# Running sums of the SSD scan: spread over the partitions by DMA from DRAM instead of by picking products

## The chip, the cores and the metric

The kernel runs on one core of a Trainium2 chip. The metric is the device time of one execution in microseconds (us). Five engines run side by side, each with its own instruction stream: TensorE (PE in the profile; PEld is its weight load), VectorE (DVE), ScalarE (ACT), GpSimd (POOL) and SyncE (SP), which here issues every DMA.

## The reference

A decoder trunk of two layers for one sequence of 256 tokens and 1024 features. Each layer is a SwiGLU feed-forward block, a token mixer and a second feed-forward block, each behind an RMSNorm that is scaled and shifted by the conditioning vector. The mixer of layer 0 is a latent attention, that of layer 1 the SSD scan (Mamba-2), in two chunks of 128 tokens, with 32 heads in 4 groups. What the change touches is the decay inside the scan:

```
a = (dt * A)                                  # per chunk, group, head, token
a_cum = jnp.cumsum(a, axis=-1)
seg = a_cum[..., :, None] - a_cum[..., None, :]
decay_ls = jnp.exp(jnp.where(causal, seg, -jnp.inf))
cb = jnp.einsum('bclgn,bcsgn->bcgls', Cc, Bc)
y_diag = jnp.einsum('bcgls,bcgkls,bcsgkp->bclgkp', cb, decay_ls, xdt)
decay_to_end = jnp.exp(a_cum[..., -1:] - a_cum)
states = jnp.einsum('bclgn,bcgkl,bclgkp->bcgkpn', Bc, decay_to_end, xdt)
```

## The kernel before

Features lie on the 128 partitions and the 256 tokens along the free dimension. Every product with a weight is made of three matmuls in float32r: weights and activations are each split into a rounded part and a remainder (`mm3`), so that a projection to 128 outputs is 8 x 3 = 24 matmuls of 256 columns.

Weights come by DMA from SyncE into five raw buffers of 1 MB (`prefetch`, line 184); a raw buffer holds two pieces for two projections. ScalarE casts a piece to float32r (`whi`, line 206) and VectorE subtracts to get the remainder (`wlo`, line 207). `piece` traces these splits two pieces ahead of the projection that uses them; five `whi` and five `wlo` buffers bound how far the engines can run ahead. Between them VectorE also forms the conditioning vectors from further weight loads (line 237).

The program is traced in Python order, and a planner then orders each engine's stream by readiness, with the trace order as priority. `order` (`keep_in_program_order`) pins an instruction behind everything traced before it on its engine, and `matmul` does so while `pin` is set, as it is inside the steps of the scan.

Work tiles: `slot` gives [128, 512] tiles from a ring of NSLOT = 30. They hold the layer's inputs (8), the second set of normalised inputs (8), the activations of a feed-forward block (22), and in the SSD layer convolution outputs, gates and scan tiles. `bank` gives one of the 8 PSUM banks.

The SSD layer (`ssd`) runs 40 projections of `win` in the order SSD_ORDER and, between them, steps of two generators. `ssd_dt` computes dt, a and the running sums; it ends with the sums by token in `nac`, `acol` and `ate`, and with the sums by head as rows in `acr`: 64 rows, where rows 0 to 31 hold a rounded value and rows 32 to 63 the remainder, with 64 rows of zeros below. Then `ssd_group` runs for each group of 8 heads in four pairs. For pair `i`, `decay` spreads the two heads' rows over all 128 partitions with two matmuls whose weight is a column of `s_pick` (a matrix that adds row h and row 32 + h), broadcast to 128 columns, into a PSUM bank. `decay_next` (line 1278) takes an exponential of the second chunk for the carried state, `decay_cut` (line 1286) takes the minimum with the own column, which masks, into a slot, and `decay_exp` (line 1297) takes four more exponentials into the `dec` tile. `times_cb` (line 1301) multiplies by C.B, `ymm` makes the products with x.dt, and `leave` (line 1316) adds the skip term. `decay(i + 1)` is traced ahead of `decay_next(i + 1)` by one step; a step is half a projection. The Exp and Silu functions need different activation tables on ScalarE, each change of which is an ACT_TABLE_LOAD.

`gate` works on a group's outputs when its scan is done and its z projections are there. Its sums of squares (line 1452) and scales (line 1463) lead to the inputs of the output projection in `down`.

Of the kernel before, what the change touches and what calls it, by code (L numbers as in the profile page):

```python
# [7 lines left out]
F32 = mybir.dt.float32  # L8
F32R = mybir.dt.float32r
# [3 lines left out]
ALU = mybir.AluOpType  # L13
# [3 lines left out]
T = 256  # L17
# [11 lines left out]
NSLOT = 30  # L29
# [35 lines left out]
class Trunk:  # L65
    def __init__(self, ctx, tc, a, out):
# [3 lines left out]
            tc.tile_pool(name="ps", bufs=8, space=bass.MemoryType.PSUM))  # L70
        self.uid = 0
# [1054 lines left out]
    def ssd_setup(self):  # L1126
        nc = self.nc
# [12 lines left out]
        self.pick = self.const([128, 32], "s_pick", F32R)  # L1140
        nc.gpsimd.memset(self.pick[64:128].bitcast(F32), 0.0)
        self.acr = self.const([128, T], "acr", F32R)
        nc.gpsimd.memset(self.acr[64:128].bitcast(F32), 0.0)
        self.order(nc.vector.tensor_tensor(out=self.pick[0:64], in0=self.ident[0:64, 0:32], in1=self.ident[0:64, 32:64], op=ALU.add))
# [17 lines left out]
    def ssd_dt(self, ps, R):  # L1162
# [27 lines left out]
        for n in (13, 9, 5, 1):  # L1190
# [13 lines left out]
        av = self.const([128, 2, 2, 32], "a_f")  # L1204
        nc.vector.tensor_tensor(
            out=av, in0=self.dt.rearrange("p c (o h) -> p c o h", o=1).broadcast_to([128, 2, 2, 32]),
            in1=self.nega.rearrange("p (c o h) -> p c o h", c=1, o=1).broadcast_to([128, 2, 2, 32]), op=ALU.mult)
        yield
        ah = self.const([128, 2, 2, 32], "a_h", F32R)
        al = self.const([128, 2, 2, 32], "a_l", F32R)  # L1210
# [6 lines left out]
        for c in range(2):  # L1217
            o = pc[:, c * 32:(c + 1) * 32]
            self.matmul(o, self.tri, ah[:, c, 0], start=True, stop=False)
            self.matmul(o, self.tri, al[:, c, 0], start=False, stop=True)  # L1220
        o = pc[:, 64:96]
        self.matmul(o, self.onesr, ah[:, 0, 0], start=True, stop=False)
        self.matmul(o, self.onesr, al[:, 0, 0], start=False, stop=True)
        pr = self.bank()
        for c in range(2):
            o = pr[0:64, c * 128:(c + 1) * 128]
            self.matmul(o, ah[:, c].rearrange("p o h -> p (o h)"), self.tri, start=True, stop=False)
            self.matmul(o, al[:, c].rearrange("p o h -> p (o h)"), self.tri, start=False, stop=True)
# [9 lines left out]
        nc.vector.tensor_copy(out=self.acr[0:64], in_=pr[0:64, 0:T])  # L1238
        nc.vector.tensor_tensor(out=self.acr[32:64], in0=pr[32:64, 0:T], in1=self.acr[32:64].bitcast(F32),
# [377 lines left out]
```

## Time and profile before

| what | value |
|---|---|
| median of 3 runs | 1082.81 us (1082.79 to 1084.13) |
| the profiled execution: its time | 1082.82 us |
| the profiled execution: its span | 1081.1 us |
| TensorE busy | 1063.7 us (98%) |
| VectorE busy | 871.5 us (81%) |
| ScalarE busy | 628.5 us (58%) |
| DMA | 259.59 MB, mean 240 GB/s |

The span runs from the first instruction to the last; some 1.7 us of the time lie around it. In the rows, L1286 is line 1286 of the kernel, `out<-in` names the tiles without their buffer numbers, `128x512 f32<-128x512 f32` are the shapes, and `xN` counts instructions. `[0.60 <-DVE dec L1301]` is idle time of the engine before the instruction and what ended it. Matmul records overlap, so their durations do not add up to time. The SSD layer lies between about 690 and 900 us of the span, the scan's four groups between 737 and 856 us.

### The profile page before, as it was taken

The numbers are of one execution on the slowest core, as the hardware profiler recorded it, in microseconds if no ns is written. First come the engines' busy times: TensorE is split into PE (matmuls) and PEld (weight loads), VectorE is DVE, ScalarE is ACT, GpSimd is POOL, SyncE is SP. The second block draws the span as 40 slices with busy tenths as digits, with TensorE's granted clock in tenths as the row PEclk, the third lists the DMA queues.
The fourth block names the chain that finished last, engine by engine and source line by source line (L and its number), as shares of the span: only waits on it lengthen the run. The fifth ranks groups of instructions, "written<-read, shape, count | busy, mean of one in ns | idle before, by whom it ended". The sixth has DMA issues, their size and how long they took to land.

```text
span 1081.1 us, 21734 instructions
## 1 busy us (share of the span) xinstructions
PE 1063.7 (98%) x8814; PEld 1046.8 (97%) x8814; DVE 871.5 (81%) x1551; ACT 628.5 (58%) x1106; POOL 42.1 (4%) x102
## 2 busy tenths in 40 slices
PE   7999999999999999999999999999999999999998
PEld 6999999999999999999999999999999899999998
DVE  5899988889989878767989886599997788756642
ACT  5564544478658444444745444498898767544431
POOL 0000000000100000100000000000211000000000
PEclk9999999999999999999999999999999999999999
DMA  8999998853366888865699987534344455566630
GB/s 342 355 357 347 336 373 298 296 202 135 117 235 226 319 313 312 300 231 211 240 346 357 343 318 250 170 142 161 114 137 156 157 179 211 203 217 215 229 132 21
DMA packets 38264, 259.59 MB, mean 240 GB/s; under 512 B 4370, under 2 KB 5522, under 8 KB 8084
## 3 DMA queue, kind: packets, MB, share of 16 engines
q1 hardware_dynamic: 38164, 258.21, 65.5%
q8 instruction: 69, 1.13, 0.4%
q14 instruction: 31, 0.25, 0.1%
HBM read 257.14 MB, written 1.05 MB: 239 GB/s over the span
## 4 chain that ended last, share of the span: by engine, by line
PE 92%; DMA 3%; DVE 3%; ACT 1%; issue 0%; SPq 0%; ACTq 0%
PE bank L295 91%; DMA raw<-in_adao_dram 3%; PE bank L300 1%; DVE raw L259 1%; DMA raw<-in_xt_dram 0%; DVE wlo L613 0%; ACT sl L808 0%; ACT t L1020 0%; DVE wlo L207 0%; ACT whi L206 0%; DVE sl L1463 0%; DVE ssq L942 0%; ACT t L937 0%; DVE mx L1015 0%; ACT sl L806 0%
## 5 line engine op out<-in xcount | busy, mean ns | idle before, releaser
L295 PE MATMUL bank<-sl,whi 128*128 128x256 f32 (+2 forms) x5360 | 957.2, 282 | 4.0 <-ACT sl L647 2.8
L295 PEld LDWEIGHTS bank<-sl,whi 128*128 128x128 f32 (+1 forms) x5360 | 819.7, 188 | 7.7 <-ACT sl L647 3.6
L295 PE MATMUL bank<-sl,wlo 128*128 128x256 f32 (+2 forms) x2680 | 747.6, 281 | 0.9 <-DVE wlo L207 0.9
L206 ACT CAST whi<-raw 128x1024 fp32r<-128x1024 f32 (+1 forms) x329 | 341.5, 1041 | 326.0 <-PE bank L295 230.8
L295 PEld LDWEIGHTS bank<-sl,wlo 128*128 128x128 f32 (+1 forms) x2680 | 504.5, 189 | 1.2 <-DVE wlo L207 1.1
L207 DVE TENSOR_TENSOR wlo<-raw,whi 128x1024 fp32r<-128x1024 f32 (+1 forms) x329 | 397.8, 1213 | 99.5 <-ACT whi L206 96.4
L237 DVE SCALAR_TENSOR_TENSOR raw<-raw,cb 128x1024 f32<-128x1024 f32 x128 | 154.4, 1218 | 14.2 <-DMA raw<-in_adaw_dram 14.1
L329 ACT CAST sl<-t 128x256 fp32r<-128x256 f32 x125 | 48.6, 404 | 23.4 <-DVE t L521 16.4
L330 DVE TENSOR_TENSOR sl<-t,sl 128x256 fp32r<-128x256 f32 x125 | 50.8, 417 | 1.0 <-ACT sl L329 0.7
L460 DVE SCALAR_TENSOR_TENSOR x<-bank,mod,x 128x256 f32<-128x256 f32 x48 | 22.9, 480 | 22.2 <-PE bank L295 21.8
L521 DVE TENSOR_TENSOR t<-t,bank 128x256 f32<-128x256 f32 x70 | 28.7, 416 | 14.8 <-PE bank L295 14.8
L1159 DVE SCALAR_TENSOR_TENSOR sl<-t,cst,sl 128x256 f32<-128x256 f32 x72 | 34.6, 490 | 0.2
L410 ACT ACTIVATE sl<-x,scol 128x256 fp32r<-128x256 f32 x40 | 20.3, 508 | 23.5 <-DVE x L460 23.4
L520 ACT ACTIVATE t<-bank 128x256 f32<-128x256 f32 x70 | 26.0, 380 | 0.0
L409 POOL CAST sl<-bspl 128x4 fp32r<-128x4 f32 x40 | 12.7, 365 | 319.2 <-PE bank L295 232.4
L440 POOL TENSOR_TENSOR rr<-rv,mhalf 128x2 f32<-128x2 f32 x11 | 12.7, 1154 | 308.0 <-DVE rv L436 308.0
L259 DVE SCALAR_TENSOR_TENSOR raw<-raw,cb 128x1024 f32<-128x1024 f32 x16 | 19.5, 1222 | 5.9 <-DMA raw<-in_adao_dram 5.9
L295 PE MATMUL bank<-whi,sl 128*128 128x384 f32 (+1 forms) x80 | 24.3, 368 | 0.0
L1297 ACT ACTIVATE dec<-sl,nac 128x128 f32<-128x128 f32 x64 | 20.5, 394 | 3.6 <-DVE sl L1286 3.5
L411 DVE SCALAR_TENSOR_TENSOR sl<-x,scol,sl 128x256 fp32r<-128x256 f32 x40 | 19.2, 480 | 4.2 <-ACT sl L410 4.1
L423 ACT ACTIVATE t<-t,mod,scol 128x256 f32<-128x256 f32 x32 | 18.2, 595 | 4.2 <-DVE t L422 4.0
L613 DVE TENSOR_TENSOR wlo<-raw,whi 128x1024 fp32r<-128x1024 f32 (+1 forms) x17 | 19.5, 1156 | 0.0
(216 smaller groups left out, 662.0 us busy)
## 6 DMA issues: line engine op xcount, KB each, us to landing
raw<-in_wgu_dram SPq DMA_DIRECT2D x80, 1024.0 KB, 5.2
raw<-in_adaw_dram SPq DMA_DIRECT2D x64, 1024.0 KB, 5.8
raw<-in_wdn_dram SPq DMA_DIRECT2D x44, 1024.0 KB, 6.2
raw<-in_win_dram SPq DMA_DIRECT2D x19, 1024.0 KB, 4.9
raw<-in_wout_dram SPq DMA_DIRECT2D x8, 1024.0 KB, 4.8
raw<-in_wop_dram SPq DMA_DIRECT2D x6, 1024.0 KB, 5.7
raw<-in_adao_dram SPq DMA_DIRECT2D x6, 1024.0 KB, 7.3
raw<-in_mwo_dram SPq DMA_DIRECT2D x4, 1024.0 KB, 4.9
```

What stands on the lines that cost most here:

```text
L206: self.nc.scalar.copy(out=hi, in_=raw)
L207: self.nc.vector.tensor_tensor(out=lo, in0=raw, in1=hi.bitcast(F32), op=ALU.subtract)
L237: nc.vector.scalar_tensor_tensor(out=w, in0=w, scalar=1.0, in1=self.cb, op0=ALU.mult, op1=ALU.mult, accum_out=self.mod[:, q, 2 * u + i:2 * ...
L259: self.order(nc.vector.scalar_tensor_tensor(out=w, in0=w, scalar=1.0, in1=self.cb, op0=ALU.mult, op1=ALU.mult, accum_out=self.mod[:, q, c]))
L295: ins = self.nc.tensor.matmul(*a, **k)
L329: self.nc.scalar.copy(out=hi, in_=src)
L330: self.nc.vector.tensor_tensor(out=lo, in0=src, in1=hi.bitcast(F32), op=ALU.subtract)
L460: nc.vector.scalar_tensor_tensor(out=self.x[m], in0=ps[:, 0:T], scalar=self.mod[:, q, m:m + 1], in1=self.x[m], op0=ALU.mult, op1=ALU.add)
L520: nc.scalar.activation(out=tg, in_=pg[:, 0:T], func=AF.Silu)
L521: nc.vector.tensor_tensor(out=tg, in0=tg, in1=pu[:, 0:T], op=ALU.mult)
L1159: nc.vector.scalar_tensor_tensor(out=dst, in0=u[:, t:t + T], scalar=cw[:, t:t + 1], in1=dst, op0=ALU.mult, op1=ALU.add)
L1297: self.order(nc.scalar.activation(out=t[:, j, 2 * c], in_=q[:, o:o + 128], func=AF.Exp, bias=self.nac[:, c, h:h + 1]))
```

## The change

The running sums by head are no longer split into a rounded value and a remainder in `acr`. `ssd_dt` writes 32 rows of them as float32 to a scratch tensor `acd` in DRAM, by a DMA from SyncE. `row_load(i)` then loads the rows of heads 2i and 2i + 1, 2 KB, broadcast to all 128 partitions, into an SBUF tile `arow`. Four such tiles exist; the first four pairs are loaded at the end of `ssd_dt`, and after the exponentials of a pair the load for the pair four later is issued. `decay` hands out the next of these tiles in place of two matmuls; `decay_cut` writes into it in place of a slot. The column sums in `ssd_dt` are made from a single copy of a. To make room, the ring of slots goes from 30 to 27.

```diff
--- before.py
+++ after.py
@@ -26,7 +26,8 @@
 RAW_BUFS = 5
 W_BUFS = 5
 AHEAD = 2
-NSLOT = 30
+NSLOT = 27
+ROWS = 4
 NDEF = 6
 ZRAW = 13
 SETUP_AT = 15
@@ -68,6 +69,7 @@
         self.p = ctx.enter_context(tc.tile_pool(name="sb", bufs=1))
         self.ps_pool = ctx.enter_context(
             tc.tile_pool(name="ps", bufs=8, space=bass.MemoryType.PSUM))
+        self.dram = ctx.enter_context(tc.tile_pool(name="dr", bufs=1, space=bass.MemoryType.DRAM))
         self.uid = 0
         self.pin = False
 
@@ -1137,11 +1139,7 @@
         nc.vector.tensor_copy(out=self.tri, in_=u)
         self.onesr = self.const([128, 128], "s_onesr", F32R)
         self.order(nc.vector.tensor_copy(out=self.onesr, in_=self.ones))
-        self.pick = self.const([128, 32], "s_pick", F32R)
-        nc.gpsimd.memset(self.pick[64:128].bitcast(F32), 0.0)
-        self.acr = self.const([128, T], "acr", F32R)
-        nc.gpsimd.memset(self.acr[64:128].bitcast(F32), 0.0)
-        self.order(nc.vector.tensor_tensor(out=self.pick[0:64], in0=self.ident[0:64, 0:32], in1=self.ident[0:64, 32:64], op=ALU.add))
+        self.acd = self.dram.tile([32, T], F32, name="acd")
 
     def conv_evac(self, ps, R, j, dst):
         nc = self.nc
@@ -1201,13 +1199,12 @@
         nc.vector.scalar_tensor_tensor(out=p, in0=p, scalar=2.0, in1=z, op0=ALU.mult, op1=ALU.mult)
         nc.vector.scalar_tensor_tensor(out=d, in0=u, scalar=0.0, in1=p, op0=ALU.max, op1=ALU.add)
         self.dt = d.rearrange("p (c h) -> p c h", c=2)
-        av = self.const([128, 2, 2, 32], "a_f")
-        nc.vector.tensor_tensor(
-            out=av, in0=self.dt.rearrange("p c (o h) -> p c o h", o=1).broadcast_to([128, 2, 2, 32]),
-            in1=self.nega.rearrange("p (c o h) -> p c o h", c=1, o=1).broadcast_to([128, 2, 2, 32]), op=ALU.mult)
-        yield
-        ah = self.const([128, 2, 2, 32], "a_h", F32R)
-        al = self.const([128, 2, 2, 32], "a_l", F32R)
+        av = self.const([128, 2, 32], "a_f")
+        nc.vector.tensor_tensor(out=av, in0=self.dt, in1=self.nega.rearrange("p (c h) -> p c h", c=1)
+                                .broadcast_to([128, 2, 32]), op=ALU.mult)
+        yield
+        ah = self.const([128, 2, 32], "a_h", F32R)
+        al = self.const([128, 2, 32], "a_l", F32R)
         nc.vector.tensor_copy(out=ah, in_=av)
         nc.vector.tensor_tensor(out=al, in0=av, in1=ah.bitcast(F32), op=ALU.subtract)
         yield
@@ -1216,16 +1213,16 @@
         pc = self.bank()
         for c in range(2):
             o = pc[:, c * 32:(c + 1) * 32]
-            self.matmul(o, self.tri, ah[:, c, 0], start=True, stop=False)
-            self.matmul(o, self.tri, al[:, c, 0], start=False, stop=True)
+            self.matmul(o, self.tri, ah[:, c], start=True, stop=False)
+            self.matmul(o, self.tri, al[:, c], start=False, stop=True)
         o = pc[:, 64:96]
-        self.matmul(o, self.onesr, ah[:, 0, 0], start=True, stop=False)
-        self.matmul(o, self.onesr, al[:, 0, 0], start=False, stop=True)
+        self.matmul(o, self.onesr, ah[:, 0], start=True, stop=False)
+        self.matmul(o, self.onesr, al[:, 0], start=False, stop=True)
         pr = self.bank()
         for c in range(2):
-            o = pr[0:64, c * 128:(c + 1) * 128]
-            self.matmul(o, ah[:, c].rearrange("p o h -> p (o h)"), self.tri, start=True, stop=False)
-            self.matmul(o, al[:, c].rearrange("p o h -> p (o h)"), self.tri, start=False, stop=True)
+            o = pr[0:32, c * 128:(c + 1) * 128]
+            self.matmul(o, ah[:, c], self.tri, start=True, stop=False)
+            self.matmul(o, al[:, c], self.tri, start=False, stop=True)
         yield
         self.nac = self.const([128, 2, 32], "nac")
         nc.vector.tensor_scalar(out=self.nac, in0=pc[:, 0:64].rearrange("p (c h) -> p c h", c=2), scalar1=-1.0,
@@ -1235,9 +1232,16 @@
                               in_=pc[:, 0:64].rearrange("p (c h) -> p c h", c=2))
         self.ate = self.const([128, 32], "ate")
         nc.vector.tensor_tensor(out=self.ate, in0=pc[:, 64:96], in1=self.nac[:, 0], op=ALU.add)
-        nc.vector.tensor_copy(out=self.acr[0:64], in_=pr[0:64, 0:T])
-        nc.vector.tensor_tensor(out=self.acr[32:64], in0=pr[32:64, 0:T], in1=self.acr[32:64].bitcast(F32),
-                                op=ALU.subtract)
+        acr = self.t1()[0:32]
+        nc.vector.tensor_copy(out=acr, in_=pr[0:32, 0:T])
+        nc.sync.dma_start(out=self.acd, in_=acr)
+        self.rows = [self.row_load(i) for i in range(ROWS)]
+
+    def row_load(self, i):
+
+        t = self.p.tile([128, 2 * T], F32, name=self.name("arow"), tag="arow", bufs=ROWS)
+        self.nc.sync.dma_start(out=t, in_=self.acd[2 * i:2 * i + 2].rearrange("h l -> (h l)").partition_broadcast(128))
+        return t
 
     def ssd_group(self, g, BT, CT, xsT):
 
@@ -1262,12 +1266,7 @@
             return t
 
         def decay(i):
-            ps = self.bank()
-            for j in range(2):
-                h = 8 * g + 2 * i + j
-                self.matmul(ps[:, j * T:(j + 1) * T], self.pick[:, h:h + 1].broadcast_to([128, 128]),
-                                 self.acr, start=(j == 0), stop=(j == 1))
-            return ps
+            return self.rows.pop(0)
 
         def decay_next(i, ps):
 
@@ -1281,13 +1280,12 @@
 
         def decay_cut(i, ps):
 
-            q = self.slot()
             h = 8 * g + 2 * i
-            nc.vector.tensor_tensor(out=q.rearrange("p (j c l) -> p j c l", j=2, c=2),
+            nc.vector.tensor_tensor(out=ps.rearrange("p (j c l) -> p j c l", j=2, c=2),
                                     in0=ps.rearrange("p (j c l) -> p j c l", j=2, c=2),
                                     in1=self.acol[:, h:h + 2, :].rearrange("p j (c o) -> p j c o", o=1)
                                     .broadcast_to([128, 2, 2, 128]), op=ALU.min)
-            return q
+            return ps
 
         def decay_exp(i, q, t):
             for j in range(2):
@@ -1296,6 +1294,8 @@
                     o = j * T + c * 128
                     self.order(nc.scalar.activation(out=t[:, j, 2 * c], in_=q[:, o:o + 128], func=AF.Exp,
                                                     bias=self.nac[:, c, h:h + 1]))
+            if 4 * g + i + ROWS < 16:
+                self.rows.append(self.row_load(4 * g + i + ROWS))
 
         def times_cb(t):
             nc.vector.tensor_tensor(out=t, in0=t, in1=bc.rearrange("p (o c l) -> p o c l", o=1, c=3)
```

## Rows read from the trace of the kernel before

**Rows 1.** The page's engines: busy us, share of span, instructions.
```profile
PE 1063.7 (98%) x8814; PEld 1046.8 (97%) x8814; DVE 871.5 (81%) x1551; ACT 628.5 (58%) x1106; POOL 42.1 (4%) x102
```

**Rows 2.** Stretches of 20 us: engines' busy us (records), granted clock, DMA share, GB/s.
```profile
740.00:760.00 20.00, 19.40 (x164) 18.07 (x163) 17.50 (x30) 19.59 (x45) 0.75 (x2) 1.00 0.46 158
...
780.00:800.00 20.00, 20.00 (x170) 18.77 (x167) 19.92 (x34) 18.78 (x41) 2.97 (x4) 1.00 0.40 132
...
820.00:840.00 20.00, 18.84 (x152) 18.14 (x151) 11.56 (x24) 19.05 (x36) 1.23 (x3) 0.96 0.31 116
```

**Rows 3.** TensorE's waits, whole span: us in total, times, longest.
```profile
PE bank L295 <- DVE t L1452: 1.2, 1, 1.2
...
PE bank L295 <- DVE wlo L207: 0.9, 1, 0.9
PE bank L295 <- DVE dec L1301: 0.6, 1, 0.6
```

**Rows 4.** TensorE's timeline, third pair of group 0: start us, us, what.
```profile
756.32 0.87 PE L295 MATMUL bank<-dec,sl 128*64 128x256 f32 x8 [0.60 <-DVE dec L1301]
```

**Rows 5.** Instructions on tile acr: ns min/median/max, first and last start us.
```profile
L295 PE MATMUL bank<-acr,s_pick x32: 277/280/384, 737.9 to 835.8; 128*128 128x256 f32 x32
L1143 POOL MEMSET acr<- x1: 307/307/307, 1.2 to 1.2; 64x256 f32 x1
...
L1239 DVE TENSOR_TENSOR acr<-bank,acr x1: 417/417/417, 735.8 to 735.8; 32x256 fp32r<-32x256 f32 x1
```

**Rows 6.** The page's costliest groups: ScalarE's weight casts.
```profile
L206 ACT CAST whi<-raw 128x1024 fp32r<-128x1024 f32 (+1 forms) x329 | 341.5, 1041 | 326.0 <-PE bank L295 230.8
```

**Rows 7.** VectorE's timeline: copy of the sums, third pair of group 0.
```profile
734.93 0.41 DVE L1238 CAST acr<-bank 64x256 fp32r<-64x256 f32 x1
...
755.22 0.95 DVE L1301 TENSOR_TENSOR dec<-dec,t 128x768 f32<-128x768 f32 x1
```

**Rows 8.** Groups by line and shape, 730-860 us: busy us, mean ns, idle.
```profile
L1297 ACT ACTIVATE dec<-sl,nac 128x128 f32<-128x128 f32 x64 | 20.5, 394 | 3.6 <-DVE sl L1286 3.5
...
L1286 DVE TENSOR_TENSOR sl<-bank,acol 128x512 f32<-128x512 f32 x16 | 10.9, 684 | 5.1 <-ACT dec L1278 5.0
...
L1278 ACT ACTIVATE dec<-bank,ate 128x128 f32<-128x128 f32 x32 | 9.9, 360 | 0.5 <-PE bank L295 0.4
```

**Rows 9.** Waits of SyncE's queue, 680 to 860 us.
```profile
SPq L184 <- DVE wlo L207: 165.5, 24, 24.1
```

**Rows 10.** Stretches where the sums are ready (columns as in rows 2).
```profile
735.50:739.00 3.50, 3.50 (x31) 3.45 (x30) 3.44 (x6) 2.01 (x4) 0.53 (x1) 1.00 0.73 281
739.00:740.00 1.00, 1.00 (x11) 1.00 (x10) 1.00 (x2) 0.99 (x2) 1.00 (x2) 1.00 0.02 8
```

**Rows 11.** DMA issues, whole span: count, KB each, median us to landing.
```profile
x<-in_x_dram SPq DMA_DIRECT2D x4, 256.0 KB, 8.7
...
out_dram<-x SPq DMA_DIRECT2D x8, 128.0 KB, 2.4
...
raw<-in_win_dram SPq DMA_DIRECT2D x1, 512.0 KB, 3.5
```

**Rows 12.** ScalarE's timeline in group 0.
```profile
739.98 0.63 ACT L1278 ACTIVATE dec<-bank,ate 128x128 f32<-128x128 f32 x2
740.50 0.60 ACT L1157 ACTIVATE sl<-t,cst 128x256 f32<-128x256 f32 x1
...
743.06 0.36 ACT L1151 COPY t<-bank 128x256 f32<-128x256 f32 x1
743.31 1.05 ACT L206 CAST whi<-raw 128x1024 fp32r<-128x1024 f32 x1
...
744.76 1.04 ACT L206 CAST whi<-raw 128x1024 fp32r<-128x1024 f32 x1
```

**Rows 13.** ScalarE's timeline: 20th activation, first feed-forward block.
```profile
134.10 0.40 ACT L329 CAST sl<-t 128x256 fp32r<-128x256 f32 x1
```

**Rows 14.** Stretch after the wait on t (columns as in rows 2).
```profile
838.00:842.00 4.00, 4.00 (x23) 4.00 (x23) 0.85 (x3) 3.96 (x6) 0.69 (x1) 0.57 0.02 4
```

## Prediction

> **What bounds the kernel now.** I read the page's table of engines first: TensorE is busy 98% of the span [rows 1]. That says TensorE sets the end, but it is a mean over stages, so the second view is the table by stretches around the scan of the SSD layer [rows 2]. There TensorE still shows 18.8 to 20 us of every 20, while ScalarE stands at 17 to 19.6 of 20. Two engines are nearly full at once, and a product taken off TensorE is worth its full time only where ScalarE and VectorE can follow. The third view is who TensorE waited for [rows 3]: three waits of 0.6, 1.2 and 0.9 us lie in the scan, on the masked decay (dec), on the sums of squares of the gate (t) and on a weight half (wlo). The fourth is the timeline of the first head group, whose third pair of heads is where TensorE waits the 0.6 us [rows 4].
>
> The price of one product is not its 280 ns record, since those overlap. In 20 us TensorE gets through 170 of them [rows 2], so one holds it for 0.117 us.
>
> **What the change takes away.** The picking products are 32 matmuls, two for each of 16 pairs of heads, from 737.9 to 835.8 us [rows 5]: 32 x 0.117 = 3.74 us of TensorE, in four groups of 8, each worth 0.94 us. Also gone: one subtraction of 0.42 us on VectorE [rows 5], 16 banks of PSUM, and two POOL memsets of the setup. These three I cost at nothing: no wait of TensorE in [rows 3] ends on POOL or on a bank's reader, the planner had put the memset to 1.2 us, far ahead of everything [rows 5], and VectorE's 0.42 us is one of 17.5 us of its stretch [rows 2].
>
> What of the 3.74 us reaches the end goes group by group.
> Groups 1 and 2 (766 to 812 us): TensorE waits for nothing there; the stretch 780 to 800 shows it 20.00 of 20. I count them in full: 2 x 0.94 = 1.87 us. VectorE is full in the same stretch at 19.92 of 20, but part of that is weight halves made ahead: of ScalarE's 326 us of idle time before its weight casts 231 us are waits for TensorE to release a buffer [rows 6], so weights run ahead by nearly all five buffers, some 4 x 24 x 0.117 = 11 us.
> Group 0: its third pair ends on ScalarE's exponentials and VectorE's product of 0.95 us at 755.22, and TensorE begins only then, after 0.60 us of waiting [rows 4, 7]. All 8 products of the group come before that point. If TensorE gets there 0.94 us sooner it waits 0.94 us longer: I count 0.
> Group 3: ScalarE is busy 19.05 of 20 in 820 to 840 and TensorE waits there, but part of the chain starts from TensorE itself. I count half, 0.47 us, with ends 0 and 0.94.
>
> **What it adds on the engines.** ScalarE's 32 first exponentials now read SBUF where they read PSUM. From PSUM they take 360 ns; the other 64, of the same size, read SBUF and take 394 [rows 8]: 32 x 0.034 = 1.1 us more on ScalarE, some 0.07 us per pair, of which perhaps 0.1 us shows at the end (the two waiting places, one pair each). VectorE's minimum of 684 ns now reads SBUF and writes in place; I cost it at 0. [...]
>
> **The new chain: write, wait, read.** The running sums are copied to SBUF by VectorE at 734.93 for 0.41 us [rows 7], so the write to DRAM can issue at about 735.4. On SyncE, which spends most of the stage waiting for a weight buffer to come free [rows 9], it stands behind the loads that are due earlier, and its packets behind theirs: the DMA engines are 73% busy from 735.5 to 739 and then 2% [rows 10], which is one 1 MB load draining. So the write lands at about 739.5 by my estimate. A 128 KB store to DRAM takes 2.4 us [rows 11], this one has a quarter of the bytes: bounds are 735.4 + 2.0 if nothing is in its way and 739 + 2.4. Row load 0 waits on SyncE for that landing. It brings 256 KB to 128 partitions. The trace has 2.4 us for 128 KB, 3.5 us for 512 KB with idle engines and 8.7 us for 256 KB in the full queue of the start [rows 11]; I take 2.8 us between the first two, since 739 to 740 is idle. Row 0 is there at 739.5 + 2.8 = 742.3, bounds 737.4 + 2.4 = 739.8 and 741.4 + 8.7 = 750.1. Before, the first exponential ran at 739.98 [rows 12]. So the chain is 2.3 us late, between on time and 10 late.
> Queued behind it on ScalarE are the group's other exponentials and all casts. But in 740.5 to 745.8 ScalarE does 0.60 + 0.36 + 1.05 + 1.04 = 3.05 us of convolution and weight casts [rows 12], which do not need the rows and which the planner can put ahead. That covers 2.3 us, so I take 0. If the order stays as it was, all of the 2.3 us lands on the third pair, at 755.2, where there is no slack.
> [...]
>
> Behind the row loads on SyncE stand weight loads. They wait for the store at most from 735.4 to about 742, and later for the exponentials of a pair (each row load reuses the buffer of four pairs before). With 11 us of weights split ahead and five raw buffers behind these, I cost it at nothing; without that lead each microsecond of delay would be one of TensorE. Later rows are asked for as the pair before in the buffer is done, a whole group or some 25 us ahead, and 4 MB over some 110 us, 38 GB/s, is hidden on DMA engines that move 116 to 158 GB/s there [rows 2].
>
> **Three work slots fewer (30 to 27).** In each SwiGLU layer 22 activations and 8 inputs are alive at the turn to the down projection: 30, by the code. With 27, the 20th and 21st activation must wait until the last projection releases inputs: in the first layer from 134.10 on ScalarE [rows 13] to about 142, 7.9 us. The same place comes four times, and three times one input of the next layer waits for the first activation to be released. The activation is needed only at the end of the down projection's first row, 6 us later, and behind it on ScalarE stand weight casts with a lead of some 10 us. I cost it at 0; bounds 0 and, with ScalarE held and VectorE not catching up, some 2 us in each of four layers, 8 us.
>
> **Sum.** 1.87 + 0 + 0.47 - 0.1 = 2.2 us gained. The profiled execution took 1082.82 us (span 1081.1 and 1.7 around it), and the median of the runs is 1082.81, so both bases give 1080.6.
>
> **Rivals.**
> A. The full gain: TensorE's clock and waits move with it, and all 32 products count: 1082.8 - 3.7 = 1079.1. For it: TensorE is 98% busy. Against: the 0.60 us wait in group 0, which 0.94 us can only lengthen. [...]
> B. The new wait takes the place of the old work: ScalarE keeps its order, row 0 is 2.3 us late and the third pair of group 0 with it: 1080.6 + 2.3 = 1082.9, no change. For it: ScalarE has 19.59 us of 20 in that stretch and no idle time to give.
> C. Slower: row 0 comes really late, because SyncE holds the store behind a weight load that still waits for its buffer, or the row load takes the 8.7 us of a full queue. Row 0 at 739.5 + 8.7 = 748.2 is 8.2 us late; 3.05 are covered, 5.2 land on group 0: 1080.6 + 5.2 = 1085.8, more with one drop of the clock. It turns the sign when the lateness not covered passes 2.2 us, so from row 0 at 745.2. The slot bound works to the same side. For it: SyncE's waits [rows 9]. Against: the load that drains until 739 is the last in the way.
> D. The rows do not spread as said, for instance because 128 reads of the same 2 KB are slow: nothing in the trace shows it. A row of 8.7 us then gives C's 1085.8, within C's chance.
>
> **How the numbers follow.** Forecast 0.40 (own range 1079.6 to 1082), A 0.15, B 0.25, C with slots and D 0.20. The measurement can tell some 0.2%, 2.2 us, from no change, so the forecast stands on that bound: of its 0.40 I give 0.25 to faster and 0.15 to same. Faster 0.15 + 0.25 = 0.40; same 0.15 + 0.25 = 0.40; slower 0.20. The range holds A, the forecast, B and the near half of C: 1078.6 to 1085.6.
>
> **What would show it.** Right: 32 matmul records fewer; TensorE's wait for dec in group 0 longer than 0.6 us by about 0.9; the first exponential between 741 and 744 with casts ahead of it; no new wait of TensorE between 130 and 210 us. Wrong: ScalarE idle for microseconds on a DMA before that exponential (B or C); ScalarE idle at some 134 us until a projection ends, with TensorE waiting for wlo later (slots); row landings over 5 us; the clock's drop gone or doubled.

## The result, and the profile after

The changed kernel takes 1095.52 us in the median of 5 runs (1093.98 to 1097.94), the kernel before 1083.68 beside it (1082.79 to 1084.58): a ratio of 1.0111, interval 1.0094 to 1.0127. It is slower by some 12 us where 2.2 us of gain were forecast, and the time lies above the range. The profiled execution took 1093.98 us (span 1092.2), 11.2 more than that of before. Its page has 8782 matmuls where there were 8814: the 32 products are gone.

Of the views named at the end of the prediction, TensorE's waits over the whole span come first (us in total, times, longest):

```profile
PE bank L297 <- DVE dec L1301: 7.2, 2, 3.7
...
PE bank L297 <- DVE t L1452: 2.4, 1, 2.4
PE bank L302 <- ACT t L1022: 2.2, 3, 1.3
```

The wait on the masked decay has grown from 0.6 to 7.2 us, that on the gate's squares from 1.2 to 2.4 [rows 3]. The third is in the attention layer, where it was 1.0; it comes back below. The stretches (columns as in [rows 2]) show where TensorE lost records, and the granted clock with it:

```profile
740.00:760.00 20.00, 16.31 (x127) 15.44 (x125) 14.51 (x22) 15.71 (x30) 0.71 (x2) 0.91 0.70 236
760.00:780.00 20.00, 16.52 (x128) 15.42 (x124) 15.70 (x25) 13.90 (x33) 4.92 (x11) 0.91 0.35 120
780.00:800.00 20.00, 20.00 (x170) 18.66 (x169) 18.61 (x36) 19.40 (x45) 1.53 (x4) 1.00 0.40 142
...
754.00:758.00 4.00, 3.95 (x22) 3.60 (x23) 3.32 (x5) 3.97 (x8) 0.00 (x0) 0.58 0.48 116
```

In the two stretches of group 0, 255 records pass where two full ones would hold 340. The last row is the 4 us after the first wait: 22 records at a mean granted clock of 0.58; in steps of 0.5 us it is 1.00 to 754.5, 0.66 to 755 and 0.50 from there to 758. By the clock, 0.42 x 4 = 1.7 us of full-speed work is lost there besides the wait. TensorE's timeline has the two waits, each ahead of a pair's products with the decay:

```profile
754.05 0.99 PE L297 MATMUL bank<-dec,sl 128*64 128x256 f32 x8 [3.69 <-DVE dec L1301]
...
766.77 0.87 PE L297 MATMUL bank<-dec,sl 128*64 128x256 f32 x8 [3.48 <-DVE dec L1301]
```

The chain of waits names what was late (start, us, what):

```profile
738.33 5.41 DMA acd<-t
743.76 4.64 DMA arow<-acd
748.47 1.28 ACT L1277
```

The store takes 5.4 us to its landing, the first row 4.6 more, and then ScalarE loads a table for 1.28 us ahead of its first exponential. SyncE's timeline shows in what company the two transfers go:

```profile
737.25 0.33 SPq L186 DMA_DIRECT2D raw<-in_win_dram  x1
738.33 0.33 SPq L1237 DMA_DIRECT2D acd<-t  x1
741.68 0.34 SPq L186 DMA_DIRECT2D raw<-in_win_dram  x1
743.76 1.76 SPq L1243 DMA_DIRECT2D arow<-acd  x4
```

A 1 MB weight load goes out 1.1 us ahead of the store, and another 2.1 us ahead of the row loads: it stands between store and rows. And ScalarE's timeline:

```profile
744.58 1.05 ACT L208 CAST whi<-raw 128x1024 fp32r<-128x1024 f32 x1 [2.04 <-PE bank L297]
745.53 0.36 ACT L1149 COPY t<-bank 128x256 f32<-128x256 f32 x1
745.93 0.60 ACT L1155 ACTIVATE sl<-t,cst 128x256 f32<-128x256 f32 x1
748.47 1.28 ACT L1277 ACT_TABLE_LOAD   x1 [1.94 <-DMA arow<-acd]
749.76 0.69 ACT L1277 ACTIVATE dec<-arow,ate 128x128 f32<-128x128 f32 x2
750.36 0.36 ACT L1423 ACTIVATE sl<-bank 128x256 f32<-128x256 f32 x1
750.63 1.03 ACT L208 CAST whi<-raw 128x1024 fp32r<-128x1024 f32 x1
...
753.59 1.04 ACT L208 CAST whi<-raw 128x1024 fp32r<-128x1024 f32 x1
...
760.62 0.70 ACT L1277 ACTIVATE dec<-arow,ate 128x128 f32<-128x128 f32 x2
```

The convolution and a cast do go ahead of the rows, and still ScalarE waits 1.94 us for a DMA. Its first exponential runs at 749.76 where it ran at 739.98 [rows 12].

**Where TensorE falls behind.** The start of the first matmul on the same weight piece, in both traces, gives how far TensorE is behind the kernel before. Single executions differ by up to 5 us at 226 us, ahead of all that differs between these kernels but the ring's length, so only the changes along a row are read. Us behind, at the place that the kernel before reaches at the time named (the last three columns are the changes from 745 to 765, from 765 to 806 and from 806 us to the end):

| kernel | 745 us | 765 us | 806 us | end | group 0 | groups 1, 2 | from group 3 on |
|---|---|---|---|---|---|---|---|
| after | 2.55 | 11.66 | 9.98 | 11.14 | +9.1 | -1.7 | +1.2 |
| 27 slots alone | 2.58 | 2.61 | 2.61 | 2.29 | 0.0 | 0.0 | -0.3 |
| group 0 by products | 3.73 | 3.69 | 2.67 | 4.52 | 0.0 | -1.0 | +1.9 |
| group 0 by products, 30 slots | -0.27 | 0.00 | -1.10 | 1.98 | +0.3 | -1.1 | +3.1 |
| sums early | 12.91 | 12.20 | 12.23 | 15.13 | -0.7 | 0.0 | +2.9 |
| rows in 30 slots | 1.76 | 11.24 | 9.46 | 12.46 | +9.5 | -1.8 | +3.0 |
| group 0 later | -1.26 | -2.46 | 0.34 | 6.81 | -1.2 | +2.8 | +6.5 |
| store and rows first | 4.28 | 5.47 | 4.64 | 5.81 | +1.2 | -0.8 | +1.2 |
| rows without store | 3.16 | 6.10 | 4.60 | 7.32 | +2.9 | -1.5 | +2.7 |
| rows first, 30 slots | -1.29 | 1.39 | -0.39 | 3.53 | +2.7 | -1.8 | +3.9 |
| first pair by products, 30 slots | 0.17 | 1.15 | 0.16 | 3.95 | +1.0 | -1.0 | +3.8 |
| groups 1 and 2 only | 1.15 | 1.43 | 0.34 | 0.74 | +0.3 | -1.1 | +0.4 |

Three things have to be kept in mind with this table. Where all groups go by rows, six products are gone by 745 us, ten by 765 and 24 by 806, so the column of group 0 holds four of them (0.47 us) and that of groups 1 and 2 fourteen (1.64 us). In "group 0 later" the scan stands elsewhere between the weight pieces: besides the products, 12 of the kernel before's matmuls are still to come at 745 us, 24 at 765 and 8 at 806. At 0.117 us each that is 1.4, 2.8 and 0.9 us, and with them the three changes of that row are +0.2, +0.9 and +5.5. And the -0.3 of "27 slots alone" holds a drop of the clock near 840 us that the kernel before has [rows 14] and this execution has not.

### The profile page after: what moved, and what is told of

It reads as the page before. It is cut to its first block, busy times and chain, and to the rows that moved or that the text cites. A ratio compares the mean times of both kernels' runs of the same rounds, so it can differ in the third digit from the quotient of the medians.

```text
span 1092.2 us, 21725 instructions
## 1 busy us (share of the span) xinstructions
PE 1063.9 (97%) x8782; PEld 1046.4 (96%) x8782; DVE 871.3 (80%) x1549; ACT 628.8 (58%) x1106; POOL 40.4 (4%) x100
## 4 chain that ended last, share of the span: by engine, by line
PE 83%; DVE 8%; DMA 4%; ACT 3%; issue 1%; POOL 0%; SPq 0%; ACTq 0%; POOLq 0%
PE bank L297 82%; DMA raw<-in_adao_dram 3%; DVE sl L1157 2%; DVE wlo L209 2%; DVE raw L261 1%; PE bank L302 1%; DVE wlo L615 1%; DMA acd<-t 0%; DMA raw<-in_xt_dram 0%; DMA arow<-acd 0%; ACT whi L208 0%; ACT L1277 0%; DVE dec L1301 0%; ACT sl L1429 0%; DVE t L424 0%
## 5 line engine op out<-in xcount | busy, mean ns | idle before, releaser
L209 DVE TENSOR_TENSOR wlo<-raw,whi 128x1024 fp32r<-128x1024 f32 (+1 forms) x329 | 397.6, 1211 | 105.3 <-ACT whi L208 103.8
L1295 ACT ACTIVATE dec<-arow,nac 128x128 f32<-128x128 f32 x64 | 20.4, 391 | 2.7 <-DVE arow L1284 2.7
L297 PE MATMUL bank<-dec,sl 128*64 128x256 f32 (+1 forms) x128 | 14.4, 346 | 7.2 <-DVE dec L1301 7.2
L302 PE MATMUL bank<-ident,t 128*96 128x128 f32 (+2 forms) x116 | 18.0, 273 | 2.2 <-ACT t L1022 2.2
```

The source lines that it names most:

```text
L209: self.nc.vector.tensor_tensor(out=lo, in0=raw, in1=hi.bitcast(F32), op=ALU.subtract)
L297: ins = self.nc.tensor.matmul(*a, **k)
L302: ins = self.nc.tensor.transpose(*a, **k)
```

## The experiments

**Theory 1**: the first row of group 0 comes late, TensorE waits for the decay twice, and each wait brings a drop of the clock. **Theory 2**: the ring of 27 slots costs its own part. **Theory 3**: the rows cost by themselves, by their traffic or by reads from SBUF.

**The smaller ring alone** (the kernel before, one constant changed):

```diff
-NSLOT = 30
+NSLOT = 27
```

> The kernel before with one edit, 27 work slots for 30; the products stay. Row-chain theory (the time goes to the late first row of group 0): no change, 1083.7 us within 2 us, TensorE's waits as before. Slot theory (ScalarE held in the feed-forward blocks): most of the 11.8 us appears here, 1090 to 1096 us, with TensorE waiting for weight halves or inputs outside the scan. Mixed: the 2.5 us by which the changed kernel is already late before the scan begins appear here, 1086 us.

Measured 1086.85 us beside 1084.06, ratio 1.0029 (1.0017 to 1.0040): slower by 2.8 us, yet not in the place that I had named. TensorE waits nowhere more in the feed-forward blocks. The one longer wait is in the attention layer, on scores' exponentials:

```profile
PE bank L300 <- ACT t L1020: 2.2, 3, 1.3
```

1.0 in two waits before, so 1.2 us. There is also a slower pace without any wait. 100 us in the first feed-forward block of the SSD layer in the kernel before (columns as in [rows 2]):

```profile
570.00:670.00 100.00, 100.00 (x852) 100.00 (x852) 83.68 (x126) 48.18 (x67) 2.21 (x8) 1.00 0.86 323
```

and with 27 slots:

```profile
570.00:670.00 100.00, 100.00 (x847) 100.00 (x846) 83.49 (x125) 47.26 (x68) 1.64 (x5) 1.00 0.87 317
```

Five matmuls fewer at the same clock and the same full engine, 5 x 0.117 = 0.6 us in 100. Kernels with 27 slots have 847 there, the changed one too, and those with 30 have 852 or 853. From 226 to 690 us every kernel with 27 slots falls back by the same 2.1 us; those with 30 by 0.1 at most, except for 0.8 in the run with group 0 later, which waits at 447 us. Which part of the ring does it is the last experiment's question.

**Group 0 by products, the others by rows** (27 slots, three row buffers):

```diff
-            return self.rows.pop(0)
+            if g:
+                return self.rows.pop(0)
+            ps = self.bank()
+            ...
+            return ps
...
-        self.rows = [self.row_load(i) for i in range(ROWS)]
+        self.rows = [self.row_load(4 + i) for i in range(ROWS)]
```

> The changed kernel, but group 0 keeps its picking products and only groups 1 to 3 take rows by DMA (three row buffers, loaded a group ahead). Row-chain theory: the 9.4 us that TensorE falls back between 742 and 773 us are gone, 0.9 us of products in group 0 come back, and groups 1 and 2 keep their 1.9 us: 1095.5 - 9.4 = 1086, 1083 if the lateness before the scan is noise. Slot theory, and the theory that the extra traffic or SyncE's queue costs: still 1093 or more.

Measured 1085.48 us, ratio 1.0017 (1.0008 to 1.0027). The 10 us are gone with the rows of group 0, and 24 products made by rows in groups 1 to 3 cost next to nothing beside the 27 slots: theory 1, against theory 3.

**The sums three places earlier** (27 slots, the rows asked for six steps ahead of group 0):

```diff
-DT_AT = 6
+DT_AT = 3
...
         self.rows = [self.row_load(i) for i in range(ROWS)]
+        for _ in range(6):
+            yield
```

> The changed kernel with the dt chain begun three projections earlier and six empty steps behind the row loads, so that group 0 stands where it stood and store and loads have 8.4 us more. Row-chain theory: row 0 is there before the first exponential is due, TensorE's two waits of 3.7 and 3.5 us for dec and the two drops of the granted clock behind them go: 1095.5 - 9.4 = 1086, or 1083 if what lies ahead of the scan is noise. Slot or traffic theory: 1093 or more.

Measured 1094.4 us, ratio 1.0097 (1.0067 to 1.0128): a miss in the total. TensorE's waits from 690 to 770 us:

```profile
PE bank L297 <- DVE a_h L1208: 2.5, 1, 2.5
PE bank L297 <- DVE a_l L1209: 0.9, 1, 0.9
PE bank L302 <- DVE t L1165: 0.6, 1, 0.6
PE bank L297 <- DVE dec L1303: 0.4, 1, 0.4
```

The wait for the decay is down to 0.4 us, as theory 1 wants, but the sums' own chain, no longer covered, makes TensorE wait 4.0 us ahead of it, and TensorE falls 6.3 us back between 675 and 745 us. The mean granted clock of this execution is 0.992, that of the kernel before 0.998.

**The rows in the slot ring, 30 slots** (all groups by rows):

```diff
-NSLOT = 27
+NSLOT = 30
...
-        t = self.p.tile([128, 2 * T], F32, name=self.name("arow"), tag="arow", bufs=ROWS)
+        t = self.slot()
```

> The changed kernel with the row tiles taken from the ring of work slots, which is 30 again; everything else as changed. Row-chain theory: no change, 1095.5 us within 2.5. Slot theory: 1084 to 1086. Mixed: some 2.5 us less, 1093.

Measured 1095.13 us, ratio 1.0104 (1.0089 to 1.0119). The attention layer's extra wait and the slow pace are gone (x853), but group 0 loses 9.5 us again, with 7.5 us of waits for the decay, and what the ring gives back is lost in group 3 (+3.0). So group 0's loss has nothing to do with the ring.

**Group 0 by products, 30 slots** (the edits of the second and the fourth experiment together, with ROWS at 4):

```diff
-            return self.rows.pop(0)
+            if g:
+                return self.rows.pop(0)
...
-        t = self.p.tile([128, 2 * T], F32, name=self.name("arow"), tag="arow", bufs=ROWS)
+        t = self.slot()
```

> Group 0 by products as before, groups 1 to 3 by rows, the row tiles taken from a ring of 30 work slots, so that neither the late first row nor the smaller ring is in it. Theory that the late first row of group 0 is the whole loss of the change: the time of the kernel before less 1.9 us (16 products of groups 1 and 2) and less up to 0.9 us (group 3), 1081 to 1082.5 us, 1083.5 if a wait in group 3 brings a drop of the clock. Rival, that the rows cost by their traffic or by ScalarE's reads from SBUF: 1084 us and more, with the loss in groups 1 to 3.

Measured 1086.56 us beside 1083.05, ratio 1.0023 (1.0011 to 1.0034): the late first row is not the whole loss. The time is the one that I had given to the rival, but groups 1 and 2 gain 1.1 us, and only group 3 and what follows lose, 3.1. TensorE's waits from 800 us on:

```profile
PE bank L297 <- DVE t L1469: 2.5, 1, 2.5
PE bank L297 <- POOL t L1469: 1.6, 1, 1.6
```

Both are waits for the gate's squares, which end on VectorE and GpSimd at the end of a group. The seventh point below comes back to it.

**Group 0 three projections later** (rows in 30 slots, the sums at their old place):

```diff
         self.rows = [self.row_load(i) for i in range(ROWS)]
+        for _ in range(6):
+            yield
```

> All four groups by rows, row tiles from a ring of 30 slots, and group 0 begins six steps of the side work (three projections, some 8.4 us) after the row loads are asked for, the running sums at their old place. Row-chain theory: the first row, some 8.4 us late in the changed kernel, is there in time, the waits of TensorE for the masked decay in group 0 (7.2 us and two drops of the clock, 9.4 us in all after the 0.9 us of fewer products) are gone, and the time falls from 1095.5 to 1081 to 1086 us (up to 1088 if the later groups now end late). Rival, that the loss of group 0 lies in the rows themselves (traffic, reads from SBUF): 1091 us or more with the waits for the decay still there.

Measured 1088.98 us, ratio 1.0048 (1.0030 to 1.0066). TensorE's waits from 738 to 776 us:

```profile
PE bank L297 <- ACT dec L1297: 1.1, 1, 1.1
PE bank L297 <- DVE dec L1303: 0.4, 1, 0.4
```

1.5 us of waits for the decay where there were 7.5, and with the postponed matmuls counted group 0 neither gains nor loses (+0.2), which by my estimate (0.9 us more of waits, 0.47 of products less) leaves no room for a drop of the clock: its 9.5 us are gone once the rows are there in time. The postponed scan ends late and gives some 6.4 us back from group 1 on, and the time is above the range that I had given for it.

**Store and rows ahead of the weight loads** (27 slots, SyncE's order written out):

```diff
-        nc.sync.dma_start(out=self.acd, in_=acr)
+        self.order(nc.sync.dma_start(out=self.acd, in_=acr))
         self.rows = [self.row_load(i) for i in range(ROWS)]
+        self.rows_first = True
...
+                if self.rows_first:
+                    self.order(ins)
```

> The changed kernel with the order on SyncE's queue written out: store, the four row loads right behind it, and only then the next weight loads. Tells how much of the first row's lateness is queueing behind weight loads. If all of it above the store and the load by themselves (2.6 us each as an unqueued store took): first row some 2 to 4 us earlier than 748.4 us, the time 1089 to 1093 us. If the wait for the landing of the store sets it whatever stands on the queue: under 1 us earlier and 1094 to 1096 us. If weight loads held up behind the store cost TensorE: a wait for a weight half after 745 us, and 1096 us or more.

Measured 1087.88 us, ratio 1.0040 (1.0025 to 1.0054): better than my best case. SyncE's timeline:

```profile
740.06 0.33 SPq L1241 DMA_DIRECT2D acd<-t  x1
741.55 1.76 SPq L1248 DMA_DIRECT2D arow<-acd  x4
743.41 0.85 SPq L187 DMA_DIRECT2D raw<-in_win_dram  x2
```

ScalarE's timeline:

```profile
744.73 1.28 ACT L1282 ACT_TABLE_LOAD   x1 [0.46 <-DMA arow<-acd]
746.03 0.69 ACT L1282 ACTIVATE dec<-arow,ate 128x128 f32<-128x128 f32 x2
```

And the store among the DMA issues from 738 to 752 us (count, KB each, median us to landing):

```profile
acd<-t SPq DMA_DIRECT2D x1, 32.0 KB, 1.5
```

The store lands 1.5 us after its issue, not 5.4, and row 0 some 3.1 us after its own (741.55 to ScalarE's start at 744.7), not 4.6. The three weight loads that go out at 734.09, 737.25 and 741.68 in the changed kernel now follow the rows, and the wait for a weight half stays at 0.9 us, as before. This is the cause in one run: of 9.1 us in group 0, 7.9 go when the two transfers don't travel behind weight loads. TensorE's wait that is left:

```profile
762.07 0.87 PE L301 MATMUL bank<-dec,sl 128*64 128x256 f32 x8 [2.29 <-DVE dec L1306]
```

**Rows that wait for no store** (they read the input x; the place on SyncE's queue written out):

```diff
-        self.nc.sync.dma_start(out=t, in_=self.acd[2 * i:2 * i + 2]...)
+        self.order(self.nc.sync.dma_start(out=t, in_=self.a["x"][i:i + 1, 0:2 * T]...))
```

> The changed kernel with the row loads reading rows of the input x of the same size in place of the scratch tensor, at their place in the written order: the store is still made, but no load waits for it. It leaves out the real running sums, so the decay is computed from other numbers. Row-chain theory: the rows land by some 742 us, the wait for the decay in group 0 falls from 7.2 to under 2 us, and the time to 1084 to 1088 us. Rival, that reading one row into 128 partitions is itself slow or loads the chip: the waits stay and the time is 1091 us or more.

Measured 1089.82 us, ratio 1.0057 (1.0036 to 1.0078): not faster than the run above, from which the two intervals don't separate it, although nobody waits for the store. From 735 to 752 us the DMA issues (count, KB each, median us to landing):

```profile
raw<-in_win_dram SPq DMA_DIRECT2D x4, 1024.0 KB, 6.5
arow<-in_x_dram SPq DMA_DIRECT2D x5, 256.0 KB, 8.7
```

and the first row by the chain of waits, and on ScalarE's timeline the end of its wait for it:

```profile
739.34 4.81 DMA arow<-in_x_dram
...
744.21 1.28 ACT L1277 ACT_TABLE_LOAD   x1 [1.06 <-DMA arow<-in_x_dram]
```

Here weight loads go out at 734.71 and 737.88, just ahead, and the first row takes 4.8 us, the middle one of five 8.7. So the queue that a transfer travels in weighs here as much as the store that the chain is spared.

**Both repairs together** (the written-out order of above and the rows in 30 slots):

```diff
+        self.order(nc.sync.dma_start(out=self.acd, in_=acr))
...
+        t = self.slot()
```

> All groups by rows, store and row loads ahead of the next weight loads, and the row tiles from a ring of 30 slots. With the queue put right the first row is about 2 us late (as in the run with 27 slots and the same queue order, where TensorE waited 2.3 us for the decay in group 0 and lost 1.8 us there). Theory that the smaller ring costs some 2.3 us of its own (waits in the attention layer 1.2, slower matmuls 1.0): the ratio to the kernel before falls from 1.0040 to 1.001 to 1.002, 1084 to 1085.5 us. Rival, that the ring costs nothing and those differences are of another origin: 1087 to 1088.5 us.

Measured 1086.34 us beside 1082.99, ratio 1.0030 (1.0014 to 1.0046): between the two cases, so it doesn't settle what the ring is worth in company of the rows. Group 0 waits 2.33 us, 2.29 with 27 slots, but this time the clock falls behind it (0.71 from 758 to 762), and group 3 and the rest lose 3.9.

**The same with the first pair of group 0 by products**:

```diff
-            return self.rows.pop(0)
+            if g or i:
+                return self.rows.pop(0)
```

> As the run above, but the first pair of heads of group 0 by two products, so that only the second pair needs a row, about 3.5 us later. Theory that what is left of the loss in group 0 is the first row's lateness of some 2 us: the wait for the decay in group 0 falls back to about 0.6 to 1.5 us, and the time to 1081 to 1083.5 us. Rival, that four pairs of rows cost ScalarE or VectorE more than they save TensorE: the wait stays above 2 us and the time is that of the run above or more.

Measured 1087.04 us, ratio 1.0027 (1.0012 to 1.0042): the wait in group 0 is still 2.0 us, and the 1.0 us that TensorE falls back there leave, by my estimate (1.4 us more of wait, 0.47 of products less), no room for a drop of the clock. ScalarE now waits for no row, and its first exponential is in time:

```profile
740.63 0.63 ACT L1298 ACTIVATE dec<-bank,ate 128x128 f32<-128x128 f32 x2
```

That is 0.65 us after the kernel before, as far as TensorE is behind. So no late row keeps this wait. By my estimate half of the 1.4 us that it is longer are the six products (6 x 0.117 = 0.7) that TensorE no longer makes ahead of it; the other half arises in the chain on ScalarE and VectorE, and its cause was not isolated.

**Rows for groups 1 and 2 only**, 30 slots:

```diff
-            return self.rows.pop(0)
+            if g in (1, 2):
+                return self.rows.pop(0)
```

> Rows for groups 1 and 2 only, where the count of products was taken in full, groups 0 and 3 by products, 30 slots. Theory that a product is worth its 0.117 us where TensorE waits for nothing: 16 of them, 1.9 us less than the kernel before, 1080.5 to 1082 us, ratio 0.998 to 0.999. If the gain is given back in group 3 whatever makes its decay, since TensorE gets there sooner and waits longer: ratio 0.9995 to 1.001, with the lag of TensorE behind the kernel before -1.9 us at the end of group 2 and about 0 after group 3.

Measured 1083.31 us beside 1082.99, ratio 0.9997 (0.9985 to 1.0010). Of the expected 1.9 us, 0.8 show in the trace from 745 to 806 us, where the 16 products lie, and the time doesn't tell them from nothing. What is missing are two waits: that for the decay in group 0 grows from 0.6 to 1.2 us, and there is a new one in group 1:

```profile
PE bank L297 <- POOL rr L442: 0.4, 1, 0.4
```

Group 3, with its products, waits 1.2 us for the squares, as before. Beside the run with group 3 by rows too (1.0023, 1.0011 to 1.0034) the intervals are just apart: rows in group 3 do cost something, though they are there in time.

**27 slots with everything else at its address** (the kernel before, an unused tile behind the ring):

```diff
-NSLOT = 30
+NSLOT = 27
...
+            f = self.const([128, 1560], "filler")
```

> The kernel before with 27 work slots, and an unused tile of the three slots' size behind them, so that every other tile lies at the address that it has in the kernel before. In every kernel with 27 slots so far TensorE gets through 847 matmuls between 570 and 670 us, in every one with 30 slots 852 or 853, and in the attention layer its wait for t is 2.2 us against 1.0. If the addresses of the other tiles make the matmuls slower: 852 or 853 in that stretch, the wait still 2.2 us, ratio about 1.0015 to 1.002. If the shorter ring itself makes both (which buffer holds what, and when it comes free): 847 and 2.2 us, ratio 1.0025 to 1.0035, as the run with 27 slots alone (1.0029). If neither is the ring: 852 and 1.0 us, ratio 1.000.

Measured 1086.04 us beside 1082.84, ratio 1.0025 (1.0013 to 1.0036), the wait 2.2 us, and:

```profile
570.00:670.00 100.00, 100.00 (x848) 100.00 (x848) 84.20 (x127) 46.63 (x65) 1.65 (x5) 1.00 0.87 321
```

So the shorter ring makes both, not the addresses of what lies behind it, and TensorE again falls back by 2.1 us from 226 to 690 us. That the other tiles lie at their old addresses is by the edit (1560 columns, three slots have 1536); no trace shows addresses.

## Why the prediction was wrong, point by point

1. **A product is worth 0.117 us where TensorE waits for nothing.** Right. The column of groups 1 and 2 holds 14 products, 1.64 us: 1.7 are measured in the changed kernel and 1.5 to 1.8 in the three others that, like it, have no new wait there. Five others gain 0.8 to 1.1: in these TensorE waits 0.4 to 0.6 us for GpSimd's `rr` in group 1.

2. **The chain write, wait, read: three terms too small, all on one side.** This is the step that failed: I had it 2.3 us late, covered, and 0 in the sum, and group 0 pays 9.1 us for it. VectorE copies the sums 3.0 us later than before [rows 7]:

```profile
737.90 0.40 DVE L1236 COPY t<-bank 32x256 f32<-32x256 f32 x1
```

So the lateness that the chain adds is 749.76 - 739.98 - 3.0 = 6.8 us, not 2.3. On the same scale (times less 3.0), the store was issued at 735.3 as I had it (735.4); it landed at 740.7, not 739.5 (+1.2), inside the upper bound of 741.4. Row 0 then took 4.64 us, not 2.8 (+1.9), and was there at 745.4. And its landing isn't the first exponential: the table load waits for the row as well, and 1.36 us pass from 748.40 to 749.76. I had set a landing against an exponential. 2.3 + 1.2 + 1.9 + 1.4 = 6.8.

3. **Where the first two came from.** I had read from [rows 10] that the DMA engines idle from 739 on. They idle for one microsecond. The kernel before itself issues weight loads there, and the next stretch is busy again (SyncE's timeline, and the columns of [rows 10]):

```profile
734.28 0.33 SPq L184 DMA_DIRECT2D raw<-in_win_dram  x1
739.43 0.33 SPq L184 DMA_DIRECT2D raw<-in_win_dram  x1
...
740.00:744.00 4.00, 4.00 (x36) 4.00 (x36) 3.95 (x7) 3.73 (x11) 0.75 (x1) 1.00 0.74 262
```

Counted from the start, these are the loads that go out at 737.25 and 741.68 in the changed kernel: the one ahead of the store, and the one between store and rows. So the company of the two transfers stood in the kernel before's own queue, and the 2.8 us for row 0 were taken for an idle stretch that isn't there. With store and rows first, the store took 1.5 us and the row 3.1, close to what I had taken for the row. No run shows the 2.0 us of my lower bound for the store: it took 1.5 us with no weight load just ahead of it, and 5.4 behind one.

4. **The cover of 3.05 us.** This step failed in kind. The convolution and a cast went ahead, as forecast, but the planner filled the place behind the rows with other casts (750.63 and 753.59 above). From the first exponential of group 0 to that of its third pair 11.82 us passed before and 10.86 after: 0.96 us caught up, not 3.05. In the run with the rows first TensorE is 4.87 us behind at 720 us, ahead of the first missing product. On that scale the first exponential is 746.03 - 739.98 - 4.87 = 1.2 us late, and VectorE's product of the third pair (760.96 against 755.22 [rows 7]) still 0.9: some 0.3 us of cover. The wait is 2.29 - 0.6 = 1.7 longer, the rest of it because TensorE gets there sooner by the products that it no longer makes, as forecast (0.94). That is rival B in kind.

5. **The clock.** Rival C named the mechanism and the sign's turn (row 0 later than 745.2; it was 745.4), but priced it at 5.2 us, "more with one drop of the clock", such as the kernel before has from 838 us on [rows 14]. Both waits were followed by a drop: the granted clock is 0.50 from 755 to 758 and from 768.5 to 771 us. Loss of group 0 = wait - 0.6 + 1.7 for each drop - 0.47 for the four products in its column: 7.2 - 0.6 + 3.4 - 0.47 = 9.5, measured 9.1. The same sum gives 1.2 with the store first (2.3, no drop; 1.2 measured), 3.3 without the store (2.7, one drop; 2.9) and 3.0 with both repairs (2.3, one drop; 2.7). It is exact without a drop, and a drop is worth 1.3 to 1.5 us of lag rather than 1.7. C, which had 0.20 together with the slots and D, was the case, and the range took in its near half only.

6. **27 slots.** I took 0 of 0 to 8, with the wait in the feed-forward blocks. Alone it costs 2.8 and 3.2 us by the medians of two runs, 2.1 of which lie between 226 and 690 us in the traces: the attention layer and a pace that no wait explains. In the changed kernel TensorE falls back 1.4 us in the attention layer (to 298 us), gets 0.5 back until 528 and loses 1.2 in the first feed-forward block of the SSD layer. No ScalarE stall at the activations showed.

7. **Group 3.** I counted half of 0.94 as gain. In every kernel that makes group 3 by rows, TensorE's wait for the gate's squares is 2.0 to 2.5 us instead of 1.2, and in every one with its products 1.2 [rows 3]. All that the group saves (0.94) goes into that wait, as in group 0, with drops of the clock (a mean of 0.72 from 840 to 852 us in the run without store, 0.86 from 836 to 848 in the kernel before) and with 30 slots a wait for GpSimd of 1.6 us or more on top: +1.2 us and more, not -0.47. Why the waits grow by more than the group saves was not isolated; traffic, ScalarE's reads and the order of its work all remain.

8. **ScalarE's reads from SBUF.** Groups by line and shape from 730 to 870 us in the changed kernel (columns as in [rows 8]):

```profile
L1284 DVE TENSOR_TENSOR arow<-arow,acol 128x512 f32<-128x512 f32 x16 | 11.1, 691 | 7.4 <-ACT dec L1277 7.2
L1277 ACT ACTIVATE dec<-arow,ate 128x128 f32<-128x128 f32 x32 | 11.0, 392 | 0.1
```

392 ns against 360 [rows 8], 32 each where I had 34, and the minimum 691 against 684. As counted; the 32 exponentials cost some 1.0 us of ScalarE's time in all.

The sum as the runs have it, for the profiled execution: start-up 1.0, the ring 2.1 and the first six products -0.6 (2.55 together at 745 us), group 0 9.1, groups 1 and 2 -1.7, the rest 1.2: 11.1 us of span. No version that was run beats the kernel before. The best the rows can do is 1 to 2 us where TensorE is full, which this measurement can't tell from no change.

## What to carry to other kernels

A transfer that replaces on-chip work has to be priced in the queue that it will stand in: look at which loads the queue issues just ahead of it and between its two halves, in the kernel before too (here the store took 5.4 us behind a weight load and 1.5 with none just ahead), and don't take a gap of 1 us between two of them for an idle stretch. Compare like with like at the end of such a chain (landing with landing, first instruction with first instruction, table load included), and count cover only where the engine's later work can't move into the place that it leaves (0.96 us of 3.05 here). A product taken away was worth 0.117 us here where TensorE waited for nothing (1.7 us for the 14 of groups 1 and 2), and nothing ahead of a point where it already waited (+0.2 us in group 0 with the rows in time).

## What the hardware showed that was not expected

- **The ring's length changed the pace of matmuls that wait for nothing.** 847 or 848 matmuls in 100 us with 27 slots, 852 or 853 with 30, at a granted clock of 1.00 and an engine full in both. Putting the other tiles back by an unused tile did not change it (848); whether it is which slot holds what, or which accesses meet, stays open.
- **The drop of the clock didn't follow from the wait's length alone.** 2.29 us of waiting brought none in one kernel, 2.33 us of the same wait did in another, and 1.16 us did in the kernel before [rows 14]. The same 1.16 us brought none with 27 slots alone, here the stretch behind the wait (columns as in [rows 2]):

```profile
840.00:844.00 4.00, 4.00 (x35) 3.72 (x36) 1.50 (x3) 3.96 (x7) 0.69 (x1) 1.00 0.01 4
```

35 records where the kernel before has 23 [rows 14]. What decides was not shown.
- **How long a 32 KB store takes to its landing goes, in these runs, by how far ahead of it the last 1 MB load went out**: 1.5 us in the three runs where that is over 13 us, 2.4 to 2.6 in the four with 2.3 to 2.5 us, and 5.2 to 5.6 in three with 1.1 us, the changed kernel among them (3.8 in the fourth, the rows without store).
